# Two transformer blocks on one core: attention weights kept in plain float32 and applied to two heads side by side

## The chip, the cores and the metric

The kernel runs on one core of one Trainium2 chip. The metric is the device time of one execution in microseconds (us), as the median of three runs: 1866.72 us (1866.5 to 1867.96). Engines are named as in the profile: PE is TensorE's matmul stream and PEld its weight loads, DVE is VectorE, ACT is ScalarE, POOL is GpSimd, SP issues DMAs.

## The reference, cut to what matters

A sequence of 512 positions with 1024 features goes through two blocks. All inputs are float32. The change touches the places where attention weights meet values:

```python
# block 1, mixer: 8 "Fox" heads of 64, 4 "Diff" heads of 128
p = softmax(where(causal, q @ k.T * scale + F_q - F_k, -inf))      # Fox, per head
o = p @ v                                                          # 512 x 64
p1 = softmax(q1 @ k1.T * scale + bias); p2 = softmax(q2 @ k2.T * scale + bias)
o = rms_norm((p1 - lam * p2) @ v) * g                              # Diff, 512 x 128
# then gates, output projection, and a mixture of 32 experts (top 2 of 8 in one of 4 groups)

# block 2, mixer: 8 "NSA" heads of 64 (4 share one key/value head) and 4 mLSTM heads of 128
o = g0 * softmax(q @ k_cmp.T + b) @ v_cmp \
  + g1 * softmax(q @ k_slc.T + b) @ v_slc \
  + g2 * softmax(q @ k_win.T + b) @ v_win                          # 31 compressed keys, 512, 512
w = exp(D - m) * (q @ k.T);  h = (w @ v) / max(|sum w|, exp(-m))   # mLSTM, causal, 512 x 128
# then output projection, cross-attention to 256 memory tokens, and a gated feed-forward layer
```

## The kernel before

**Products.** Most matrix products run in the type float32r (`F32R`); such a product shows in the profile as one record. To come near float32, an operand is split in two: `hi` is the value rounded to float32r (an ACT instruction, L138), `lo` is the rest (a DVE subtraction, L145, which has to wait for `hi`). `mm3` (L152 to L154) then adds three products: hi·hi, hi·lo and lo·hi. A plain float32 operand needs no split; its product shows in the profile as two records for one instruction of the code. `hidden` (L804) issues 2 x 8 x 2 = 32 plain float32 products for each of 16 expert blocks, so 512, and its group on the page counts 1024.

**Attention.** A head works in four blocks of 128 queries; block `i` has keys 0 to 128(i+1). `softmax_rows` (L237, L239) leaves rows `sx` (queries on partitions). `transposer` (L254) turns them: for key block `j` it transposes the 4-j row blocks into one PSUM tile `tr` of 512, 384, 256 or 128 columns, and splits that into `pTh` and `pTl`. `finish` then applies them to the values. A Fox or NSA head (L441, L1489) puts the split values side by side (`v` hi in columns 0 to 63, lo in 64 to 127) as the stationary operand and streams `pTh` and `pTl` of each `j`: eight products of 512, 512, 384, 384, 256, 256, 128 and 128 columns. The result has the hi part on PSUM partitions 0 to 63 and the lo part on 64 to 127, so ACT copies one half out (`ou`), DVE adds the other, and the sum is split for the output projection (`oah`/`oal`, `yAh`/`yAl`). A Diff or mLSTM head (L475/L477, L1786/L1788) has 128-wide values; for each (i, j) one product streams 256 columns (hi and lo values) and a second 128, and ACT copies one half (`on`), DVE adds the other.

**Order.** Block 1's attention is a loop over head groups in which softmax blocks of one head, transposes of the head before and units of the next head's projection (`fill`) alternate. Block 2's is `run_tasks`: a task is one NSA head with one branch (`b` = 0 selected, 1 window), 16 in all, then four mLSTM cells. The NSA accumulator `o` is opened in `finish` of branch 0 (compressed branch first, L1483, then selected) and closed by branch 1. A scheduler in the framework then sets each engine's order; engines run theirs strictly in order. PSUM has four `mm` tiles, two `sc` (scores) and two `tr` (transposes). In block 2's attention stage the `lo` part of projection weights (`wl`, L219) and the mLSTM's convolution (`cy`, `mq`) run on POOL. mLSTM starts with `sel`, four small DVE copies (L1730) that a product (L1751) needs.

**Stages of the trace that the change touches** (us from the span's start): Fox 85 to 171, Diff 171 to 258, NSA 1090 to 1246, mLSTM 1246 to 1312.

Of the kernel before, what the change touches and what calls it, by code (L numbers as in the profile page):

```python
# [94 lines left out]
class Builder:  # L95
# [218 lines left out]
    def mixer1(self, x_dram, outer, before_gates, before_out):  # L314
        nc, tc, a = self.nc, self.tc, self.a
        w_in = a["w_in"][0]
        with ExitStack() as st:
# [10 lines left out]
            va = big.tile([P, NT, 8, 2, 64], F32R, tag="va_ob", name="va")  # L328
# [15 lines left out]
            with ExitStack() as sa:  # L344
# [75 lines left out]
                class Fox:  # L420
# [13 lines left out]
                    def finish(s, pT):  # L434
                        h, rr = s.h, slice(64 * s.r, 64 * s.r + 64)
                        o = ps.tile([P, S], F32, tag="mm", name="mm")
                        for j in range(NT):
                            sg = slice(self.SEG[j], self.SEG[j] + S - P * j)
                            v = va[:, j, h].rearrange("p a d -> p (a d)")
                            for m in range(2):  # L440
                                nc.tensor.matmul(o[:, P * j:], lhsT=v, rhs=pT[m][:, sg], start=j + m == 0,  # L441
                                                 stop=j == NT - 1 and m == 1)
# [1539 lines left out]
```

## Time and profile before

| | us |
|---|---|
| median of three runs | 1866.72 |
| the profiled execution's own time | 1868.54 |
| its span (first to last instruction) | 1866.7 |
| PE busy / PEld busy | 1768.0 / 1249.7 |
| DVE busy / ACT busy / POOL busy | 892.3 / 632.1 / 101.2 |
| mean granted TensorE clock | 0.976 of 2.4 GHz |

The span is 1.8 us shorter than the execution's own time; the profiled execution is 1.8 us longer than the median. "Busy" of an engine is the union of its records. A matmul record lasts longer than the engine needs for it: neighbours overlap, so rates are read from start to start, or from a group's union of busy time divided by its count. Over the whole span PE is busy 95% and DVE 48%; in the four stages above DVE is busy 64 to 90% of the time and ACT 47 to 81%.

### The profile page before, as it was taken

The numbers are of one execution on the slowest core, as the hardware profiler recorded it, in microseconds if no ns is written. First come the engines' busy times: TensorE is split into PE (matmuls) and PEld (weight loads), VectorE is DVE, ScalarE is ACT, GpSimd is POOL, SyncE is SP. The second block draws the span as 40 slices with busy tenths as digits, with TensorE's granted clock in tenths as the row PEclk, the third lists the DMA queues.
The fourth block names the chain that finished last, engine by engine and source line by source line (L and its number), as shares of the span: only waits on it lengthen the run. The fifth ranks groups of instructions, "written<-read, shape, count | busy, mean of one in ns | idle before, by whom it ended". The sixth has DMA issues, their size and how long they took to land. (4 is left out here: it accounts for less than half of the span.)

```text
span 1866.7 us, 22058 instructions
## 1 busy us (share of the span) xinstructions
PE 1768.0 (95%) x8295; PEld 1249.7 (67%) x8295; DVE 892.3 (48%) x2194; ACT 632.1 (34%) x1235; POOL 101.2 (5%) x100
## 2 busy tenths in 40 slices
PE   7999999999999999999998998889999999999998
PEld 5677777887655343333337876657787798888886
DVE  6499964335412221212107678866675553333224
ACT  4387742322100000000005568654354432323221
POOL 0000000011000000000001034200000000000000
PEclk9999999999999999999999999888999999999999
DMA  6322245346799999999977431101332233332321
GB/s 209 79 59 55 57 167 165 100 167 249 280 411 416 416 416 416 416 417 414 417 294 239 142 96 40 46 29 66 104 114 79 63 108 97 95 102 91 101 92 45
DMA packets 188987, 343.78 MB, mean 184 GB/s; under 512 B 14324, under 2 KB 136661, under 8 KB 172110
## 3 DMA queue, kind: packets, MB, share of 16 engines
q1 hardware_dynamic: 174768, 309.49, 45.9%
q0 software_dynamic: 8080, 25.07, 3.8%
q10 hardware_dynamic: 6030, 7.78, 1.2%
q8 instruction: 66, 1.08, 0.2%
q14 instruction: 43, 0.35, 0.1%
HBM read 330.74 MB, written 18.37 MB: 187 GB/s over the span
## 5 line engine op out<-in xcount | busy, mean ns | idle before, releaser
L219 DVE TENSOR_TENSOR wl<-wr,wh 128x1024 fp32r<-128x1024 f32 (+1 forms) x167 | 202.1, 1212 | 290.8 <-ACT wh L138 288.4
L138 ACT ACTIVATE wh<-wr 128x1024 fp32r<-128x1024 f32 (+1 forms) x178 | 185.9, 1050 | 434.0 <-PE mm L153 188.5
L152 PE MATMUL mm<-hTh,wh 128*128 128x512 f32 (+1 forms) x832 | 328.7, 395 | 0.0
L153 PE MATMUL mm<-hTl,wh 128*128 128x512 f32 (+1 forms) x832 | 322.8, 388 | 0.0
L154 PE MATMUL mm<-hTh,wl 128*128 128x512 f32 (+1 forms) x832 | 321.1, 386 | 0.4 <-DVE wl L219 0.4
L804 PE MATMUL mm<-we,xs 128*64 128x512 f32 x1024 | 241.4, 594 | 0.0
L154 PEld LDWEIGHTS mm<-hTh,wl 128*128 128x128 f32 x832 | 159.3, 191 | 29.9 <-DVE wl L219 0.8
L152 PEld LDWEIGHTS mm<-hTh,wh 128*128 128x128 f32 x832 | 159.1, 191 | 30.0 <-issue 3.8
L804 PEld LDWEIGHTS mm<-we,xs 128*64 128x64 f32 x1024 | 89.9, 137 | 129.3 <-issue 125.2
L153 PEld LDWEIGHTS mm<-hTl,wh 128*128 128x128 f32 x832 | 159.5, 192 | 24.4 <-issue 0.7
L856 PE MATMUL sc<-we,hT 128*64 128x512 f32 x512 | 142.3, 606 | 1.7 <-issue 1.7
L842 DVE SCALAR_TENSOR_TENSOR h<-mm,rsl,h 128x512 f32<-128x512 f32 x16 | 12.0, 750 | 178.8 <-PE mm L804 178.8
L856 PEld LDWEIGHTS sc<-we,hT 128*64 128x64 f32 x512 | 45.6, 138 | 76.8 <-issue 71.6
L239 ACT ACTIVATE sx<-sx,mn 128x384 f32<-128x384 f32 (+3 forms) x128 | 71.3, 557 | 23.9 <-DVE mn L237 23.5
L859 ACT COPY yt<-sc 128x512 f32<-128x512 f32 x16 | 9.4, 585 | 196.2 <-PE sc L856 196.2
L145 DVE TENSOR_TENSOR pTl<-tr,pTh 128x512 fp32r<-128x512 f32 (+3 forms) x136 | 66.3, 494 | 13.7 <-ACT pTh L138 13.3
L138 ACT ACTIVATE pTh<-tr 128x512 fp32r<-128x512 f32 (+3 forms) x136 | 59.0, 441 | 37.4 <-PE tr L254 31.6
L254 PE MATMUL tr<-ident,sx 128*128 128x128 f32 x320 | 62.3, 286 | 8.3 <-DVE pTl L145 4.9
L770 DVE TENSOR_TENSOR xg<-tr,gmoe 128x512 f32<-128x512 f32 x32 | 22.1, 690 | 97.8 <-PE tr L768 97.8
L254 PEld LDWEIGHTS tr<-ident,sx 128*128 128x128 f32 x320 | 40.4, 144 | 23.9 <-DVE pTl L145 8.9
L768 PE MATMUL tr<-x1h,oh 128*128 128x512 f32 x128 | 53.9, 421 | 0.3 <-DVE xs L792 0.3
L792 ACT COPY xs<-tr 128x512 f32<-128x512 f32 x16 | 9.4, 586 | 130.5 <-PE tr L780 130.4
(616 smaller groups left out, 3085.8 us busy)
## 6 DMA issues: line engine op xcount, KB each, us to landing
we<-in_w_dram SPq DMA_DIRECT2D x126, 1024.0 KB, 15.0
we<-in_w_dram SPq DMA_DIRECT2D x132, 512.0 KB, 14.3
wr<-in_w_in_dram SPq DMA_DIRECT2D x60, 512.0 KB, 3.9
wr<-in_w_gate_up_dram SPq DMA_DIRECT2D x44, 512.0 KB, 3.8
wr<-in_w_down_dram SPq DMA_DIRECT2D x22, 512.0 KB, 3.4
wr<-in_w_o_dram SPq DMA_DIRECT2D x8, 512.0 KB, 3.2
wr<-in_w_xkv_dram POOLq DMA_DIRECT2D x8, 512.0 KB, 7.7
yc<-ybuf SPq DMA_DIRECT2D x8, 512.0 KB, 8.4
```

The costliest lines, as they stand in the source:

```text
L138: self.nc.scalar.activation(out, src, AF.Copy if isinstance(scale, float) else AF.Identity, scale=scale)
L145: nc.vector.tensor_sub(lo, src, hi.bitcast(F32))
L152: mm(out, lhsT=lhs[0], rhs=rhs[0], start=start, stop=False)
L153: mm(out, lhsT=lhs[0], rhs=rhs[1], start=False, stop=False)
L154: mm(out, lhsT=lhs[1], rhs=rhs[0], start=False, stop=stop)
L219: next(self.lo_engines).tensor_sub(lo, raw, hi.bitcast(F32))
L239: nc.scalar.activation(s[:, :n], s[:, :n], AF.Exp, bias=mn, scale=-1.0, accum_out=rs)
L254: nc.tensor.transpose(pt[:, (i - j) * P:(i - j + 1) * P], rows[i][:, j * P:(j + 1) * P], self.ident)
L768: nc.tensor.matmul(pt, lhsT=oh[:, t], rhs=self.x1[m][:, t, c], start=t + m == 0, stop=t == NT - 1 and m == 1)
L770: nc.vector.tensor_mul(xg[:, c], pt, self.gmoe[:, c])
L804: self.nc.tensor.matmul(z[rr], lhsT=xs[:, k, rr], rhs=we[4 * m + 2 * (k // 4) + r][k % 4], start=k == 0, stop=k == KC - 1)
L856: nc.tensor.matmul(zs[hf][rr], lhsT=hT[:, k, rr], rhs=we[8 + 2 * (k // 2) + r][k % 2][:, hf * 512:hf * 512 + 512], start=k == 0, stop=k == 3)
```

## The change

The two mixers drop the split of the attention weights and of the values.

- `transposer32` copies each `tr` tile once, as float32, into `pT`: on ACT for j = 0 and 2, on DVE for j = 1 and 3. `pTh`, `pTl` and their eight split instructions a head go.
- The values `va`, `vb`, `vs`, `vc`, `mv` are copied once in float32.
- Fox and NSA: `finish` of an even head only keeps its `pT`. `finish` of the odd head calls `apply_pair`: for each `j` two plain float32 products with a stationary operand of 128 x 64, the even head's into PSUM partitions 0 to 63 and the odd head's into 64 to 127 of one tile. The tile is split for the output projection as it stands; `ou` and its addition go. The compressed branch does the same (`cp`, 31 x 64).
- Diff and mLSTM: one plain float32 product of 128 columns for each (i, j); the `on` copy and addition go (Diff scales from PSUM; mLSTM copies on DVE).
- `pT` has 3 buffers in block 1, 4 in NSA, 2 in mLSTM (before, `pTh` and `pTl` had 2 each).

```diff
+    def transposer32(self, rows, pool, ps, bufs):
+        nc = self.nc
+        out = pool.tile([P, 1280], F32, tag="pT", name="pT", bufs=bufs)
+        def step(j):
+            n = S - P * j
+            pt = ps.tile([P, S], F32, tag="tr", name="tr")
+            for i in range(j, NT):
+                nc.tensor.transpose(pt[:, (i - j) * P:(i - j + 1) * P], rows[i][:, j * P:(j + 1) * P], self.ident)
+            (nc.scalar.copy, nc.vector.tensor_copy)[j % 2](out[:, self.SEG[j]:self.SEG[j] + n], pt[:, :n])
+        step.out = out
+        return step
+
+    def apply_pair(self, o, vs, pTs, start=True, stop=True):
+        for j in range(NT):
+            for r in range(2):
+                self.nc.tensor.matmul(o[64 * r:64 * r + 64, P * j:], lhsT=vs[r](j),
+                                      rhs=pTs[r][:, self.SEG[j]:self.SEG[j] + S - P * j], start=start and j == 0,
+                                      stop=stop and j == NT - 1)
...
-            va = big.tile([P, NT, 8, 2, 64], F32R, tag="va_ob", name="va")
+            va = big.tile([P, NT, 8, 64], F32, tag="va_ob", name="va")
...
                     for t in range(NT):
-                        z = accs[t].rearrange("p (h d) -> p h d", d=wide)
-                        self.split(v[:, t, :, 0], v[:, t, :, 1], z)
+                        (nc.scalar.copy, nc.vector.tensor_copy)[t % 2](
+                            v[:, t], accs[t].rearrange("p (h d) -> p h d", d=wide))
...
                     def finish(s, pT):
-                        h, rr = s.h, slice(64 * s.r, 64 * s.r + 64)
+                        pTs = s.box.setdefault("pT", [])
+                        pTs.append(pT)
+                        if s.r == 0:
+                            return
                         o = ps.tile([P, S], F32, tag="mm", name="mm")
-                        for j in range(NT):
-                            sg = slice(self.SEG[j], self.SEG[j] + S - P * j)
-                            v = va[:, j, h].rearrange("p a d -> p (a d)")
-                            for m in range(2):
-                                nc.tensor.matmul(o[:, P * j:], lhsT=v, rhs=pT[m][:, sg], start=j + m == 0,
-                                                 stop=j == NT - 1 and m == 1)
-                        u = wk.tile([64, S], F32, tag="on", name="ou", bufs=1)
-                        nc.scalar.copy(u, o[64:])
-                        nc.vector.tensor_add(u, o[:64], u)
-                        self.split(oa[0][rr, h // 2], oa[1][rr, h // 2], u)
+                        self.apply_pair(o, [lambda j, h=s.h + r - 1: va[:, j, h] for r in range(2)], pTs)
+                        self.split(oa[0][:, s.h // 2], oa[1][:, s.h // 2], o)
...
                                 c0 = self.SEG[j] + P * (i - j)
-                                nc.tensor.matmul(o[:, :2 * P], lhsT=aT[0][:, c0:c0 + P],
-                                                 rhs=vb[:, j, h].rearrange("p a d -> p (a d)"), start=j == 0, stop=False)
-                                nc.tensor.matmul(o[:, :P], lhsT=aT[1][:, c0:c0 + P], rhs=vb[:, j, h, 0],
-                                                 start=False, stop=j == i)
-                            nc.scalar.copy(on[:, i], o[:, P:2 * P])
-                            nc.vector.tensor_add(on[:, i], o[:, :P], on[:, i])
-                            nc.vector.tensor_scalar_mul(on[:, i], on[:, i], s.inv1[:, i:i + 1])
+                                nc.tensor.matmul(o[:, :P], lhsT=aT[:, c0:c0 + P], rhs=vb[:, j, h], start=j == 0,
+                                                 stop=j == i)
+                            nc.vector.tensor_scalar_mul(on[:, i], o[:, :P], s.inv1[:, i:i + 1])
...
-                            trs = self.transposer(prev.rows, wk, pst)
+                            trs = self.transposer32(prev.rows, wk, pst, 3)
...
-                    hi = wk.tile([31, S], F32R, name="cph", bufs=1)
-                    lo = wk.tile([31, S], F32R, name="cpl", bufs=1)
-                    self.split(hi, lo, pt[:31])
-                    s.head["pc"] = (hi, lo)
+                    s.head["pc"] = wk.tile([31, S], F32, name="cp", bufs=3)
+                    nc.scalar.copy(s.head["pc"], pt[:31])
...
                 def finish(s, pT):
+                    s.pT = pT
+                    if s.h % 2 == 0:
+                        return
+                    heads = (tasks[2 * s.h - 2 + s.b], s)
                     if s.b == 0:
                         o = s.head["o"] = ps.tile([P, S], F32, tag="mm", name="mm")
-                        v = vc[:, s.g].rearrange("p a d -> p (a d)")
-                        for m in range(2):
-                            nc.tensor.matmul(o, lhsT=v, rhs=s.head["pc"][m], start=m == 0, stop=False)
+                        for r, t in enumerate(heads):
+                            nc.tensor.matmul(o[64 * r:64 * r + 64], lhsT=vc[:, s.g], rhs=t.head["pc"], start=True,
+                                             stop=False)
                     o = s.head["o"]
...
+                    self.apply_pair(o, [lambda j: vs[:, j, 2 * s.b + s.g]] * 2, [t.pT for t in heads], False, s.b == 1)
                     if s.b == 1:
-                        u = wk.tile([64, S], F32, tag="sx", name="ou", bufs=SN)
-                        nc.scalar.copy(u, o[64:128])
-                        nc.vector.tensor_add(u, o[0:64], u)
-                        rr = slice(64 * (s.h % 2), 64 * (s.h % 2) + 64)
-                        self.split(yA[0][rr, s.h // 2], yA[1][rr, s.h // 2], u)
+                        self.split(yA[0][:, s.h // 2], yA[1][:, s.h // 2], o)
...
-            self.run_tasks(tasks, 1.25, 0, wk, pst, before)
+            self.run_tasks(tasks, 1.25, 0, wk, pst, before, 4)
...
-                        nc.tensor.matmul(o[:, :2 * P], lhsT=aTr[0][:, c0:c0 + P],
-                                         rhs=mv[:, j, h].rearrange("p a d -> p (a d)"), start=j == 0, stop=False)
-                        nc.tensor.matmul(o[:, :P], lhsT=aTr[1][:, c0:c0 + P], rhs=mv[:, j, h, 0],
-                                         start=False, stop=j == i)
-                    nc.scalar.copy(on[:, i], o[:, P:2 * P])
-                    nc.vector.tensor_add(on[:, i], o[:, :P], on[:, i])
+                        nc.tensor.matmul(o[:, :P], lhsT=aTr[:, c0:c0 + P], rhs=mv[:, j, h], start=j == 0, stop=j == i)
+                    nc.vector.tensor_copy(on[:, i], o[:, :P])
```

Line numbers differ in the changed kernel; its transposes are L269, its copies L270, `apply_pair` L280, the compressed product L1500, its `sel` L1739 and the product that reads it L1760.

**Order, first place.** PE at the end of a Fox head, kernel before: the eight products of one head (`pTh`, `pTl` with `va`) stand together, behind a unit of projection and ahead of the next head's scores (`ka`, `kb`).

```order
L441 MATMUL mm<-pTh,va 128x512
L441 MATMUL mm<-pTl,va 128x512
L441 MATMUL mm<-pTh,va 128x384
L441 MATMUL mm<-pTl,va 128x384
L441 MATMUL mm<-pTh,va 128x256
L441 MATMUL mm<-pTl,va 128x256
L441 MATMUL mm<-pTh,va 128x128
L441 MATMUL mm<-pTl,va 128x128
L416 MATMUL sc<-ka,qa_243 128x128
```

The same place in the changed kernel, at the end of the first odd head ("x2" is the even head's product and then the odd head's):

```order
L154 MATMUL mm<-hTh,wl 128x512
L280 MATMUL mm<-pT,va 64x512 x2
L280 MATMUL mm<-pT,va 64x384 x2
L280 MATMUL mm<-pT,va 64x256 x2
L280 MATMUL mm<-pT,va 64x128 x2
L440 MATMUL sc<-ka,qa_243 128x128
L440 MATMUL sc<-kb,qb 128x128
```

All four Fox pairs stand together like this, and so do three of the four window pairs of NSA.

**Order, second place.** PE in NSA, the compressed and selected branch of one head, kernel before (`cph`/`cpl` with `vc`, then `pTh`/`pTl` with `vs`; `kk` are scores):

```order
L1483 MATMUL mm<-cph,vc 128x512
L1483 MATMUL mm<-cpl,vc 128x512
L1489 MATMUL mm<-pTh,vs 128x512
L1489 MATMUL mm<-pTl,vs 128x512
L1489 MATMUL mm<-pTh,vs 128x384
L1489 MATMUL mm<-pTl,vs 128x384
L1489 MATMUL mm<-pTh,vs 128x256
L1455 MATMUL sc<-kk_7065,qs 128x128
L1455 MATMUL sc<-kk_7066,qs 128x128
L152 MATMUL mm<-hTh,wh 128x512
L1489 MATMUL mm<-pTl,vs 128x256
```

The selected branch of the second pair in the changed kernel (`vt` and `ce` are transposes of other work):

```order
L1500 MATMUL mm<-cp,vc 64x512 x2
L280 MATMUL mm<-pT,vs 64x512
L1396 MATMUL tr<-ident,vt 128x128 x4
L269 MATMUL tr<-ident,sx 128x128 x2
L280 MATMUL mm<-pT,vs 64x512
L280 MATMUL mm<-pT,vs 64x384 x2
L280 MATMUL mm<-pT,vs 64x256
L1459 MATMUL tr<-ident,ce 31x128 x4
L269 MATMUL tr<-ident,sx 128x128
L280 MATMUL mm<-pT,vs 64x256
L280 MATMUL mm<-pT,vs 64x128
L1468 MATMUL sc<-kk_6859,qs 128x128
```

Other work stands between the even head's and the odd head's product of the same columns. Over all of NSA this happens twelve times: six times at 512 columns (two of them in L1500), once at 384, twice at 256, three times at 128.

**Order, third place.** DVE from the end of NSA into mLSTM, kernel before (`pTl` is the last split, `qkl` the split of queries and keys):

```order
L145 TENSOR_TENSOR pTl<-tr,pTh 128x128
L1494 TENSOR_TENSOR ou<-mm,ou 64x512
L145 TENSOR_TENSOR yAl<-ou,yAh 64x512
L1727 TENSOR_SCALAR gnorm<-vec 128x4
L1730 COPY sel<-ident 4x128 x4
L147 SCALAR_TENSOR_TENSOR qkl<-mq,qkh 128x512 x4
```

and the changed kernel:

```order
L270 COPY pT<-tr 128x384
L270 COPY pT<-tr 128x128
L1736 TENSOR_SCALAR gnorm<-vec 128x4
L1739 COPY sel<-ident 4x128 x4
L145 TENSOR_TENSOR yAl<-mm,yAh 128x512
L147 SCALAR_TENSOR_TENSOR qkl<-mq,qkh 128x512 x4
```

`sel` now stands ahead of the last head's output split. On PE, where L1751 followed the last NSA product at once, 18 projection products (six units of L152 to L154) now stand between that product and L1760. PE's, DVE's and ACT's order outside the two attention parts and the first few projection products stays as it was, as does SP's but for two weight loads that stand one place later; POOL's has one `wl` a few places earlier.

## Rows read from the trace of the kernel before

**Rows 1.** Windows: Fox, Diff, NSA, mLSTM; busy by engine, PEclk, DMA share, GB/s.
```profile
85.00:171.00 86.00, 81.99 (x419) 65.59 (x418) 77.06 (x207) 69.94 (x154) 0.00 (x0) 1.00 0.22 56
171.00:258.00 87.00, 80.87 (x401) 63.51 (x401) 74.93 (x277) 58.37 (x165) 0.00 (x0) 0.96 0.24 70
1090.00:1246.00 156.00, 136.65 (x741) 106.33 (x739) 134.13 (x397) 114.02 (x285) 46.94 (x29) 0.97 0.16 45
1246.00:1312.00 66.00, 64.72 (x265) 43.75 (x265) 42.03 (x151) 31.04 (x88) 3.33 (x7) 0.79 0.19 70
```

**Rows 2.** Waits of PE in NSA (us in total, times, longest).
```profile
PE mm L1489 <- DVE pTl L145: 7.1, 6, 2.2
PE tr L254 <- DVE pTl L145: 4.1, 4, 2.4
```

**Rows 3.** Groups by form, DVE: xcount | busy us, mean ns | idle before, releaser.
```profile
L145 DVE TENSOR_TENSOR pTl<-tr,pTh 128x512 fp32r<-128x512 f32 x40 | 27.2, 685 | 8.9 <-ACT pTh L138 8.6
...
L145 DVE TENSOR_TENSOR pTl<-tr,pTh 128x256 fp32r<-128x256 f32 x32 | 13.2, 414 | 1.0 <-ACT pTh L138 1.0
...
L849 DVE COPY hT<-tr 128x512 f32<-128x512 f32 x16 | 11.0, 688 | 10.1 <-PE tr L847 10.1
...
L145 DVE TENSOR_TENSOR yAl<-ou,yAh 64x512 fp32r<-64x512 f32 x8 | 7.6, 949 | 1.1 <-ACT yAh L138 1.0
...
L1494 DVE TENSOR_TENSOR ou<-mm,ou 64x512 f32<-64x512 f32 x8 | 5.5, 682 | 5.7 <-ACT ou L1493 5.7
...
L480 DVE TENSOR_TENSOR on<-mm,on 128x128 f32<-128x128 f32 x16 | 4.4, 282 | 1.4 <-ACT on L479 1.4
```

**Rows 4.** Groups by form, ACT.
```profile
L138 ACT ACTIVATE pTh<-tr 128x384 fp32r<-128x384 f32 x32 | 15.4, 482 | 4.9 <-PE tr L254 4.8
...
L138 ACT ACTIVATE pTh<-tr 128x128 fp32r<-128x128 f32 x32 | 8.7, 271 | 10.7 <-PE tr L254 10.1
...
L138 ACT ACTIVATE yAh<-ou 64x512 fp32r<-64x512 f32 x8 | 5.0, 626 | 0.9 <-DVE ou L1494 0.7
...
L1493 ACT COPY ou<-mm 64x512 f32<-64x512 f32 x8 | 4.7, 582 | 5.3 <-PE mm L1489 5.3
...
L479 ACT COPY on<-mm 128x128 f32<-128x128 f32 x16 | 3.8, 262 | 0.6 <-PE mm L477 0.6
```

**Rows 5.** Timeline of PE, end of a Fox head: start, us, instruction.
```profile
165.57 0.39 PE L441 MATMUL mm<-pTh,va 128*128 128x512 f32 x1
165.80 0.39 PE L441 MATMUL mm<-pTl,va 128*128 128x512 f32 x1
...
166.67 0.27 PE L441 MATMUL mm<-pTl,va 128*128 128x128 f32 x1
```

**Rows 6.** Groups by form, PE: plain float32 at 64 and at 128 columns.
```profile
L804 PE MATMUL mm<-we,xs 128*64 128x512 f32 x1024 | 241.4, 594 | 0.0
...
L1266 PE MATMUL mm<-wr,we 128*128 128x512 f32 x32 | 14.4, 592 | 0.0
```

**Rows 7.** Timeline of PE, experts: change between 128*64 and 128*128.
```profile
657.59 0.59 PE L856 MATMUL sc<-we,hT 128*64 128x512 f32 x1
658.11 0.50 PE L768 MATMUL tr<-x1h,oh 128*128 128x512 f32 x1
...
659.38 0.39 PE L768 MATMUL tr<-x1l,oh 128*128 128x512 f32 x1
659.70 1.07 PE L856 MATMUL sc<-we,hT 128*64 128x512 f32 x2
```

**Rows 8.** Tile view of sx, DVE at L1470: count, min/median/max ns, first and last start.
```profile
L1470 DVE TENSOR_SCALAR sx<-sx,nrs x48: 275/470/2535, 1096.8 to 1238.1; 128x128 f32<-128x128 f32 x16, 128x256 f32<-128x256 f32 x16, 128x512 f32<-128x512 f32 x16
```

**Rows 9.** Waits of PE in mLSTM.
```profile
PE mm L1751 <- DVE sel L1730: 3.1, 1, 3.1
```

**Rows 10.** Windows: first two parts of mLSTM.
```profile
1246.00:1270.00 24.00, 23.48 (x52) 13.64 (x53) 10.36 (x31) 6.64 (x14) 0.00 (x0) 0.50 0.04 11
1270.00:1294.00 24.00, 23.85 (x120) 16.78 (x119) 17.05 (x61) 13.33 (x41) 0.00 (x0) 1.00 0.13 45
```

More of the change, by code (lines that the diff above doesn't have):

```diff
@@ L352, in mixer1 @@
                 aug_k = cc.tile([P, S], F32, name="aug_k")
-                vb = cc.tile([P, NT, 4, 2, P], F32R, name="vb")
+                vb = cc.tile([P, NT, 4, P], F32, name="vb")
                 def values(c0, v, wide):
@@ L525, in mixer1 @@
                         self.drain()
-                trs = self.transposer(prev.rows, wk, pst)
+                trs = self.transposer32(prev.rows, wk, pst, 3)
                 for j in range(NT):
@@ L1201, in post_norm, with run_tasks @@
         return done
-    def run_tasks(self, tasks, slots, more, wk, pst, before):
+    def run_tasks(self, tasks, slots, more, wk, pst, before, bufs):
         prev, self.credit = None, 0
@@ L1209, in run_tasks @@
                 cur.start()
-            trs = self.transposer(prev.rows, wk, pst) if prev is not None else None
+            trs = self.transposer32(prev.rows, wk, pst, bufs) if prev is not None else None
             for i in range(NT):
@@ L1285, in mixer2 @@
         mq = rp.tile([P, 4, S], F32, name="mq")
-        mv = rp.tile([P, NT, 4, 2, P], F32R, name="mv")
+        mv = rp.tile([P, NT, 4, P], F32, name="mv")
         with ExitStack() as sa:
@@ L1289, in mixer2 @@
             gates = cc.tile([P, NT, 24], F32, name="gates")
-            vs = cc.tile([P, NT, 4, 2, 64], F32R, name="vs")
+            vs = cc.tile([P, NT, 4, 64], F32, name="vs")
             kk = [[cc.tile([P, S], F32R, name="kk%d%d" % (b, m)) for m in range(4)] for b in range(2)]
             kcp = [cc.tile([P, 64], F32R, name="kcp%d" % m) for m in range(2)]
-            vc = cc.tile([31, 2, 2, 64], F32R, name="vc")
+            vc = cc.tile([31, 2, 64], F32, name="vc")
             tabs = [cc.tile([P, 896], F32, name="tab%d" % i) for i in range(2)]
@@ L1336, in mixer2 @@
                 nc.vector.tensor_copy(gi[:, t], accs[t][:, 256:288])
-                z = accs[t][:, 0:256].rearrange("p (g d) -> p g d", d=64)
-                self.split(vs[:, t, :, 0], vs[:, t, :, 1], z)
+                nc.scalar.copy(vs[:, t], accs[t][:, 0:256].rearrange("p (g d) -> p g d", d=64))
             nc.scalar.activation(gates, gi[:, :, 0:24], AF.Exp, scale=-1.0)
@@ L1381, in done @@
                         nc.tensor.transpose(pt[:, t * P:(t + 1) * P], vt[:, t * P:(t + 1) * P], self.ident)
-                    self.split(mv[:, :, h, 0], mv[:, :, h, 1], pt.rearrange("p (t d) -> p t d", d=P))
+                    nc.scalar.copy(mv[:, :, h], pt.rearrange("p (t d) -> p t d", d=P))
                 self.queue_proj(lambda: w, hT, ps, done)
@@ L1665, in compress @@
             ov = o[:31, :P].rearrange("p (g d) -> p g d", d=64)
-            self.split(out[:, :, 0], out[:, :, 1], ov)
+            nc.vector.tensor_copy(out, ov)
     def mlstm_gates(self, pool, keep, gi, out):
@@ L1811, in mlstm @@
         cells = [Cell(h) for h in range(4)]
-        self.run_tasks(cells, 1, 1, wk, pst, before)
+        self.run_tasks(cells, 1, 1, wk, pst, before, 2)
         cells[3].after()
```

6 lines of the change are left out of this document (removed).

## Prediction

> **What bounds the kernel now.** I read the busy times of the four stages first [rows 1]. In none of them is PE without idle time: 4.0 us in Fox, 6.1 in Diff, 19.4 in NSA, 1.3 in mLSTM (86.00 - 81.99 and so on). The reader is to see that DVE is nearly as full as PE in the first three (77.1, 74.9 and 134.1 us) and that the granted clock is 0.79 in mLSTM, against 0.96 to 1.00 elsewhere. Then the waits of PE in NSA: 11.2 of the 19.4 us end on `pTl`, the second half of a split [rows 2]. Then mLSTM: PE waits 3.1 us for `sel` [rows 9], and the 24 us from there on run at 0.50, that is 1.2 GHz, with PE busy 23.5 of them; the 24 after that run at 1.00, 2.4 GHz [rows 10]. So NSA waits on a chain through ACT and DVE, and mLSTM's first part is PE at half clock.
>
> **What goes from DVE and ACT.** One task's split costs DVE four subtractions; two of them become copies at the same price (688 ns for a 512-column copy out of PSUM, 685 for the subtraction), two go, those of 512 and 256 columns: 0.685 + 0.414 = 1.10 us [rows 3]. ACT keeps the 512 and 256 and loses the 384 and 128: 0.482 + 0.271 = 0.75 us [rows 4]. The output of a pair took DVE 2 x (0.68 + 0.68) and ACT 2 x (0.58 + 0.63); one split of 0.68 and 0.63 stays, so 2.04 and 1.8 us go [rows 3, 4]. By stage, DVE and ACT:
> - Fox, 8 tasks, 4 pairs: 8.8 + 8.2 = 17.0 us, and 6.0 + 7.2 = 13.2.
> - Diff, 4 tasks and 16 `on` additions of 0.28 and copies of 0.26: 4.4 + 4.5 = 8.9, and 3.0 + 4.2 = 7.2.
> - NSA, 16 tasks, 4 pairs, and the second halves of 8 `cpl` and 4 `mv` at the 512-column price: 17.6 + 8.2 + 8.2 = 34.0, and 12.0 + 7.2 = 19.2.
> - mLSTM, 4 cells: DVE 4.4 (the additions become copies), ACT 3.0 + 4.2.
> DVE falls by a quarter in NSA. The value copies before the heads save about as much again as one task each; projection products run beside them, so they count as nothing.
>
> **What changes on PE.** A Fox head's eight products now take from 165.57 to 166.67 and one more short one, 1.16 us; one of 512 columns starts 0.23 after the last [rows 5]. So a pair costs 2.32. The new form stands in the experts: 512 products of 128 x 64 by 512 columns fill 1024 records in 241.4 us, 0.47 us a product, while one with 128 columns takes two records of 14.4/32 = 0.45, 0.90 us [rows 6]. Two neighbouring halves of the array thus run side by side. A pair of 512 columns costs 0.94, and the 1280 columns of a pair of heads 2.36 us. Each change of shape costs 0.32 against 0.23 on the way in and 0.52 against about 0.45 on the way out [rows 7], 0.09 and 0.07, so 2.52 with both: 0.2 more than before, 0.8 over four Fox pairs. From below, with free changes of shape and a pair at the 0.90 of one full-width product, it would be 2.25, 0.07 less than before; from above, halves that do not overlap cost 1280/512 x 2 x 0.90 = 4.5.
>
> In NSA the order breaks twelve of these pairs. A broken pair costs one product more than a whole one: 6 x 0.9 + 0.66 + 2 x 0.45 + 3 x 0.22 = 7.6 us, and 24 changes of shape x 0.08 = 1.9. The eight pairs cost 8 x 0.2 = 1.6 more; the compressed branch, 16 products of 0.23 and eight detours into the 31-row shape at 0.16, 5.0, becomes four pairs of 0.94 and about 0.3, 4.1. PE's work in NSA grows by 7.6 + 1.9 + 1.6 - 0.9 = 10 us.
>
> A Diff or mLSTM step (i, j) streams 256 + 128 columns at 0.23 for 512, so at least 0.17 us; the new product has two records of 128 columns, 0.90/4 = 0.225 [rows 5, 6]. That is up to 0.05 more, over 40 steps 2 us in either stage, or nothing if steps this short took 0.225 before as well; I take nothing, as both stages have that much idle time or more slack at half clock.
>
> **What of it lies on the path, stage by stage.**
> Fox: PE idles 4.0 us, and DVE had 9 us to spare; with 17 less it is late less often. Half of the idle time, less 0.8 of PE work: -1, bounds -4 and +2.
> Diff: 6.1 us idle, and the last head has no projection beside it, so there each of its four `on` copies and additions, 0.54 us, stands on the chain: -2.2, and a `pT` ready 0.4 to 0.7 us earlier. I take -3, bounds -6 and +2.
> NSA: of the 11.2 us that end on `pTl` one wait of 2.4 [rows 2] is DVE held up elsewhere (a 128- to 512-column scaling that takes 0.275 to 2.535 us [rows 8]); I keep it and let 8.8 go. Of the other 8.2 us of idle time half goes with a quarter less on DVE: -4. PE's 10 us come on top, but the breaks are where the order puts other work because the odd head's `pT` is not there yet, so PE would have stood still in part of them; I count 7. Sum -6, bounds -19 (all idle gone, breaks free) and +10 (nothing gone).
> mLSTM: `sel` now stands on DVE ahead of the output split, `ou` and its addition are gone from the chain, and 18 projection products, 18 x 0.23 = 4.2 us, cover it on PE: the 3.1 us go. Without that stop I expect the clock to stay at 2.4 GHz. The 23.5 us of PE work at 0.50 would need 11.7 at 1.00; DVE's 10.4 us in that stretch fit into 12 only if nothing waits, so I take -8 of the 11.7. Together -11, bounds -15 and -1 (the clock falls all the same).
> [...]
>
> Sum: -1 - 3 - 6 - 11 = -21. The profiled execution takes 1868.54 us, 1.8 over its span and 1.8 over the median; 1868.5 - 21 = 1847.5, and less 1.8 for the median 1845.7. I predict 1846.
>
> **The rivals.**
> 1. The clock falls in mLSTM anyway. For it: Diff and NSA have lowered stretches too (0.96 and 0.97 [rows 1]), and NSA's longest waits in these rows are 2.2 and 2.4 us [rows 2]. Against it: plain float32 products keep PE busy longer there than before. It takes back the 8 us: 1854.
> 2. NSA stays as long as it is, because DVE is held up by single slow instructions, not by its load. For it: 2.535 us where 0.275 is possible [rows 8]; POOL is busy 46.9 us in that stage [rows 1]. Against it: 11.2 us of PE's idle time end on an instruction that the change removes. NSA +4 instead of -6: 1856. [...]
> 3. Slower: the two halves of a pair do not run side by side here, since their stationary operands change with every product. Each pair of heads then costs 4.5 in place of 2.36. Fox: 4 x 2.2 more PE work on a PE whose idle 4 us end on other things, +8. NSA: the breaks cost nothing more, but eight pairs cost 2.2 more each and four compressed ones up to 0.9: 10 - 7.6 + 17 + 2 = 21, less the 8.8 of `pTl` waits, +12. With Diff's -3 and mLSTM's -11 the sum is +6: 1873. It decides once the odd half starts more than 0.4 us after the even one. Against it: the experts change both operands with every product too, and pay 0.47 [rows 6].
> 4. More: without the wait at each tile, PE runs NSA with little idle (-17) and Fox loses its 4 us: 1832.
>
> **How the numbers follow.** Forecast 0.45, its own range 1837 to 1853; the clock 0.2; NSA unchanged 0.13, and with the clock too 0.05 (1864); slower 0.1; more 0.07. Leaving out the slower case and the top of the double one, the range is 1830 to 1865. What this kernel's runs can tell from no change is 0.2%, 3.7 us. Faster by more has all cases that end below 1863: 0.83; within it, part of the double case and the edge of the slower one, 0.07; slower 0.10.
>
> **What the profile after would show.** The two halves of an `apply_pair` product start within some ns and the pair takes 0.9 us at 512 columns; in NSA the split ones 0.9 each. DVE in NSA near 100 us, ACT near 95, PE's need up by 10. No wait for `sel`, and PEclk near 1.00 in mLSTM, which ends within some 55 us. Stages outside the four keep their lengths. Wrong it is if PE idles as much in NSA as before, if the clock in mLSTM stands at 0.5, or if a pair takes 1.8.

## The result, and the profile after

The changed kernel takes 1840.27 us (four runs, 1837.61 to 1842.04) against 1866.7 us: a ratio of 0.9854, 95% interval [0.984, 0.9867], 26.4 us faster. The forecast was 1846, 20.7 us faster, with a range of 1830 to 1865. The profiled execution has a span of 1840.3 us against 1866.7.

The stages are cut here at the last product of Fox and of NSA, since the change also moves projection work from one stage to the next. First the kernel before, then the changed one; the columns are those of [rows 1]: Fox, Diff, NSA, mLSTM.

```profile
85.00:183.40 98.40, 94.04 (x479) 75.28 (x478) 88.79 (x252) 78.67 (x177) 0.00 (x0) 1.00 0.21 54
183.40:258.10 74.70, 68.92 (x343) 53.92 (x342) 63.20 (x233) 49.64 (x142) 0.00 (x0) 0.95 0.25 75
1090.00:1243.40 153.40, 136.62 (x741) 106.33 (x739) 132.90 (x395) 112.81 (x283) 46.94 (x29) 0.97 0.15 42
1243.40:1313.60 70.20, 65.69 (x272) 44.61 (x272) 44.52 (x159) 33.18 (x94) 3.81 (x7) 0.81 0.23 80
```

```profile
85.40:177.80 92.40, 91.72 (x473) 68.59 (x471) 76.17 (x223) 66.59 (x150) 0.00 (x0) 1.00 0.22 58
177.80:246.60 68.80, 65.54 (x349) 51.57 (x348) 56.97 (x210) 44.40 (x117) 0.00 (x0) 1.00 0.23 65
1082.00:1225.40 143.40, 132.54 (x727) 93.68 (x725) 100.78 (x344) 96.66 (x239) 47.17 (x29) 0.96 0.15 45
1225.40:1286.00 60.60, 60.60 (x282) 42.39 (x282) 39.89 (x136) 27.56 (x68) 2.75 (x5) 0.89 0.22 77
```

Fox and Diff together fall from 173.1 to 161.2 us, NSA from 153.4 to 143.4, mLSTM from 70.2 to 60.6. Some is given back: the gates behind Diff take 144.7 us instead of 142.0, the work behind mLSTM 1.2 more, and 1.2 in all is lost in block 1's start and ahead of NSA. -11.9 - 10.0 - 9.6 + 5.1 = -26.4. DVE in NSA stands at 100.8 us (132.9 before) and ACT at 96.7 (112.8); "near 100" and "near 95" were forecast. Over the four stages PE's idle time (the length less its busy time) falls from 31.4 to 14.8 us, by 16.6, and the time at a granted clock of 0.50 from 44.4 to 23.9 us, worth another 10 if half of it is counted as lost: 26.8 of the 31.5 us. That half is an estimate, here and below: products of 512 columns that follow one another start 0.43 us apart at 0.50 (before, from 1249.12) and 0.23 at 1.00 (after, from 1227.78), a little less than twice.

A pair of Fox heads on PE, timeline (start, duration, instruction), with the product ahead of it and the one behind it:

```profile
114.38 0.39 PE L154 MATMUL mm<-hTh,wl 128*128 128x512 f32 x1
114.70 2.37 PE L280 MATMUL mm<-pT,va 128*64 128x512 f32 x16
117.00 0.33 PE L440 MATMUL sc<-ka,qa 128*128 128x128 f32 x1
```

The 16 records of the pair take 2.30 us from start to start, and the way in 0.32 for 0.23. With both changes of shape that is 2.39, against 2.32 for two heads before [rows 5] and 2.52 in the forecast. So the two halves of a pair do run side by side, the second starting 6 ns behind the first (single records at 114.697 and 114.703), and the slower case is out.

One broken pair in NSA, same view:

```profile
1147.76 1.07 PE L1500 MATMUL mm<-cp,vc 31*64 31x512 f32 x4
1148.77 1.07 PE L280 MATMUL mm<-pT,vs 128*64 128x512 f32 x2
1149.77 0.66 PE L1396 MATMUL tr<-ident,vt 128*128 128x128 f32 x4
1150.27 0.38 PE L269 MATMUL tr<-ident,sx 128*128 128x128 f32 x2
1150.58 1.72 PE L280 MATMUL mm<-pT,vs 128*64 128x512 f32 x8
1152.22 0.62 PE L1459 MATMUL tr<-ident,ce 128*31 128x128 f32 x4
```

The even head's 512 columns run alone, 1.00 us with the change to the shape of the transposes. But from 1150.58 the odd head's 512, both 384 and the even head's 256 take 1.64 us together: 896 columns in the odd half beside 640 in the even one, where a whole pair takes 2.30 x 896/1280 = 1.61 for 896 in both. The late half runs its old product while the other has gone on to its next one: single records of the trace put the start of the odd head's 512 columns at 1150.577 and that of the even head's 384 at 1150.584. Here the break at 512 columns thus costs its 1.00 us once, and those behind it are partly caught up.

Waits of PE in NSA after (us in total, times, longest), against [rows 2]:

```profile
PE sc L1468 <- DVE mn L237: 3.6, 3, 2.5
PE tr L1459 <- DVE ce L1452: 2.9, 3, 1.6
PE tr L269 <- ACT sx L1481: 2.5, 2, 1.5
PE tr L269 <- DVE pT L270: 1.6, 1, 1.6
```

The 11.2 us on `pTl` are gone, and 10.6 us stand on other instructions: scores' minima `mn`, the compressed branch's `ce`, scalings `sx`, the copy `pT`. On `mn` PE had waited 2.3 us and on `ce` 1.2 before as well.

mLSTM after in three windows:

```profile
1225.40:1233.00 7.60, 7.60 (x31) 5.13 (x31) 5.40 (x11) 4.86 (x9) 0.00 (x0) 1.00 0.14 38
1233.00:1246.70 13.70, 13.70 (x31) 7.56 (x30) 5.39 (x17) 3.61 (x8) 0.00 (x0) 0.50 0.10 38
1246.70:1286.00 39.30, 39.30 (x222) 29.70 (x223) 29.10 (x109) 19.09 (x52) 2.75 (x5) 1.00 0.28 97
```

No wait for `sel` is left; PE is busy for all of the 60.6 us. Yet the granted clock stands at 0.50 for 13.7 of them, where [rows 10] had 24. What PE did before it fell, from NSA's last transposes on:

```profile
1222.57 0.55 PE L269 MATMUL tr<-ident,sx 128*128 128x128 f32 x3
1223.05 2.37 PE L280 MATMUL mm<-pT,vs 128*64 128x512 f32 x14
1225.34 0.49 PE L152 MATMUL mm<-hTh,wh 128*128 128x512 f32 x1
...
1229.41 0.40 PE L154 MATMUL mm<-hTh,wl 128*128 128x512 f32 x1
1229.74 1.12 PE L1760 MATMUL mm<-aT,sel 4*128 4x512 f32 x2
...
1232.70 0.54 PE L152 MATMUL mm<-hTh,wh 128*128 128x512 f32 x1
1233.04 0.62 PE L153 MATMUL mm<-hTl,wh 128*128 128x512 f32 x1
```

The product at 1233.04 lasts 0.62 us, where one like it took 0.40 at 1229.41. No transpose stands between NSA's last ones, at 1222.57, and the fall.

### The profile page after: what moved, and what is told of

Read it like the earlier page. It is cut to its first block, busy times and chain, and to the rows that moved or that the text cites. A ratio compares the mean times of both kernels' runs of the same rounds, so it can differ in the third digit from the quotient of the medians.

```text
span 1840.3 us, 21813 instructions
## 1 busy us (share of the span) xinstructions
PE 1754.1 (95%) x8295; PEld 1226.6 (67%) x8295; DVE 834.3 (45%) x2070; ACT 590.9 (32%) x1110; POOL 101.5 (6%) x100
## 5 line engine op out<-in xcount | busy, mean ns | idle before, releaser
L152 PE MATMUL mm<-hTh,wh 128*128 128x512 f32 (+1 forms) x832 | 327.9, 395 | 0.7 <-ACT wh L138 0.7
L154 PE MATMUL mm<-hTh,wl 128*128 128x512 f32 (+1 forms) x832 | 318.7, 383 | 0.6 <-DVE wl L219 0.6
L154 PEld LDWEIGHTS mm<-hTh,wl 128*128 128x128 f32 x832 | 158.1, 190 | 31.0 <-DVE wl L219 1.1
L152 PEld LDWEIGHTS mm<-hTh,wh 128*128 128x128 f32 x832 | 158.2, 190 | 30.2 <-issue 3.3
L269 PE MATMUL tr<-ident,sx 128*128 128x128 f32 x320 | 60.5, 282 | 5.0 <-ACT sx L1481 2.5
L269 PEld LDWEIGHTS tr<-ident,sx 128*128 128x128 f32 x320 | 41.7, 144 | 23.2 <-ACT sx L1481 3.2
L784 PE MATMUL tr<-x1l,oh 128*128 128x512 f32 x128 | 51.7, 404 | 0.0
L876 DVE COPY yt<-sc 128x512 f32<-128x512 f32 x16 | 11.1, 691 | 76.8 <-PE sc L872 76.8
```

The lines of the kernel that those rows point to most:

```text
L152: mm(out, lhsT=lhs[0], rhs=rhs[0], start=start, stop=False)
L154: mm(out, lhsT=lhs[1], rhs=rhs[0], start=False, stop=stop)
L269: nc.tensor.transpose(pt[:, (i - j) * P:(i - j + 1) * P], rows[i][:, j * P:(j + 1) * P], self.ident)
L784: nc.tensor.matmul(pt, lhsT=oh[:, t], rhs=self.x1[m][:, t, c], start=t + m == 0, stop=t == NT - 1 and m == 1)
```

## The experiments

**Which stage gives what.** Three kernels carry one part of the change each: block 1's attention, block 2's mixer, and NSA alone.

```diff
+            va = big.tile([P, NT, 8, 64], F32, tag="va_ob", name="va")        # va, vb, Fox and Diff
+            self.run_tasks(tasks, 1.25, 0, wk, pst, before, 4)                # NSA and
+        self.run_tasks(cells, 1, 1, wk, pst, before, 2)                       # mLSTM
+            self.run_tasks(tasks, 1.25, 0, wk, pst, before, 4)                # NSA alone
```

Each comes with the lines of the change that belong to it.

> Only block 1's attention (Fox, Diff) is changed; block 2 stays as it was. Theory: the gain of each block stands for itself. In the traces the changed block 1 ends 11.9 us earlier, of which the gates give 2.8 back: 1866.7 - 9 = 1858. Rival: the 2.8 us lost in the gates belong to a clock that falls once in any case, so the gain of block 1 alone is 6 or less, or 12: 1861 or 1855.

Measured 1860.95, ratio 0.9965 [0.9952, 0.9977]: 6.5 us, 4.3 to 9.0. Its profile ends the gates 8.4 us early, mLSTM 9.6 and the program 8.5. The rival's gain of 6 fits as well as the theory's 9; its 12 is out.

> Only block 2's mixer (NSA, mLSTM) is changed. Theory: NSA and mLSTM together end 19.6 us earlier than before in the traces, of which 1.2 are given back by 1320: 1866.7 - 18 = 1849. Rival: block 2 gains only because it starts under another clock history: under 14 us, 1853 or more.

Measured 1848.6, ratio 0.9904 [0.987, 0.9938]: 17.9 us, 12 to 24. The four executions lie at 1841.59, 1843.95 (mean granted clock 0.985) and 1853.25, 1853.68 (0.978): how long the clock is down differs between executions of one kernel, and that goes with some 10 us. The theory's 18 us is met by the median, but the interval does not shut out the rival's 14. The two parts add up to 24.4, which agrees with the whole's 26.4 within their intervals.

> Only NSA is changed (weights once, pairs); Fox, Diff and the mLSTM cells stay as they were. Theory: NSA's own part is about 13 us (its stretch 158.5 to 141.0 us with 18 products moved out of it, 4.2), and the stop before mLSTM goes with it, since the output split is what sel stood behind: with the fall in mLSTM 1852, without it 1843. Rival, of the prediction: NSA's own part is 6: 1849 to 1860.

Measured 1849.93, ratio 0.9905 [0.9889, 0.992], 17.7 us: as much as all of block 2, and within the rival's range. In its profile NSA alone takes 143.8 us from its first scores to its last product on the values, against 152.6 before; 12 projection products moved out (2.8 us) are part of that, so NSA's own part is 6, as the rival has it, 3.4 of them the clock (3.4 us at 0.50 in place of 10.2). The larger rest lies behind NSA, where PE no longer waits for `sel`. What the mLSTM cells themselves save cannot be read from the medians, since the kernel with all of block 2 spreads over 12 us. In the two profiles, each with 6.8 us at 0.50 in NSA and mLSTM, these stages take 203.8 us without the changed cells and 197.1 with them, so it is some 6 us.

**The stop ahead of mLSTM.** The kernel before, with nothing changed but:

```diff
-        sel = cc.tile([4, 4, P], F32, name="sel")
-        for h in range(4):
-            nc.vector.tensor_copy(sel[:, h], self.ident[:4, h:h + 1].to_broadcast([4, P]))
...
-                nc.tensor.matmul(s.ab, lhsT=sel[:, s.h], rhs=aT, start=True, stop=True)
+                nc.tensor.matmul(s.ab, lhsT=self.ident[:4, s.h:s.h + 1].to_broadcast([4, P]), rhs=aT,
+                                 start=True, stop=True)
```

> The kernel before, with mLSTM's row product reading the identity's column by a broadcast, so that PE no longer waits 3.1 us for sel. Theory of the prediction: the stop also brought the clock down; without it 3.1 + 8 us go: 1856. Rival: the clock falls in mLSTM all the same, as it does for 13.7 us in the changed kernel without any wait: only the 3.1 us and the shorter fall go, at most (24 - 14)/2 = 5 more, 1858 to 1864; if nothing of the fall goes, 1863.5.

Measured 1851.74, ratio 0.9917 [0.99, 0.9933]: 15.5 us, 12 to 19, so the rival is out. The windows of NSA and mLSTM:

```profile
1085.00:1240.50 155.50, 139.81 (x738) 108.76 (x737) 132.10 (x393) 112.70 (x281) 47.25 (x29) 0.95 0.14 41
1240.50:1294.20 53.70, 52.10 (x273) 38.13 (x272) 44.18 (x155) 32.96 (x95) 3.81 (x7) 1.00 0.26 90
```

mLSTM runs at 1.00, but the clock stands at 0.50 for 10.2 us late in NSA (1218.9 to 1229.1), where the kernel before has no fall. Over both stages, 209.2 us for 223.6, the time at 0.50 goes from 37.5 to 17.1 us: the 3.1 us of the stop and half of these 20.4 are 13.3 of the 14.4. One wait of 3.1 us was thus worth more than half of what the whole change brings; its share and the clock's cannot be told apart by the medians.

> The changed kernel, with mLSTM's row product over 128 rows (124 of them zero) in place of 4, in the same time. Theory: the clock falls 3.3 us after the first such product because PE has little to do in those 1.1 us; with all rows it stays at 2.4 GHz in mLSTM, -5 to -7: 1834. Rival: it is the short products with 64 rows, or NSA's end before it; the clock falls all the same, 1840.

```diff
+        aT = keep.tile([P, S], F32, name="aT")        # was [4, S]; rows 4 to 127 zero
+        nc.vector.memset(aT, 0.0)
...
+            nc.vector.tensor_copy(sel[:, h], self.ident[:, h:h + 1].to_broadcast([P, P]))
```

Measured 1834.67, ratio 0.9824 [0.9807, 0.9841]. Its mLSTM has no fall:

```profile
1227.70:1281.50 53.80, 53.80 (x282) 39.12 (x282) 39.62 (x135) 27.38 (x68) 2.74 (x5) 1.00 0.23 84
```

That is what was expected, but the row product stayed as it was in two kernels below, those with the odd head first and with `wl` on DVE, and their mLSTM windows stand at 0.97 and 1.00. So it is not shown that the four rows bring the fall.

**Load or chain.** After each copy out of `tr`, the other engine reads the tile once more, for nobody:

```diff
+            if j % 2 == 0:
+                nc.vector.tensor_sub(dead[:, :n], pt[:, :n], out[:, self.SEG[j]:self.SEG[j] + n])
+            else:
+                nc.scalar.copy(dead[:, :n], pt[:, :n])
```

> The changed kernel, with the split's second half put back as work that nobody reads: DVE subtractions of 512 and 256 columns and ACT copies of 384 and 128, per transposed head. It loads DVE with 1.10 us a head again (17.6 in NSA, half of what it saves there) and holds the PSUM tile as long as before; PE waits for none of it. Theory, load: half of the gain outside mLSTM's start goes, +8 to +12, 1850. Rival, chain: what counted was that a product waited for ACT and then DVE; 0 to +3, 1841 to 1843.

Measured 1849.17, ratio 0.9892 [0.9874, 0.991]: 7 to 9 us of the gain are given back, by the ratios and by the medians. Its NSA:

```profile
1087.70:1242.00 154.30, 142.03 (x739) 98.46 (x737) 116.25 (x376) 105.63 (x271) 46.82 (x29) 0.94 0.14 42
```

DVE has 15.5 us more than in the changed kernel, and the stage is 10.9 us longer. The loss is near what the load theory gave and well over the chain theory's 0 to 3. How it comes about is not shown: of the 10.9 us, 3.0 are 13 projection products that stand in NSA and not behind it, 3.4 are the clock (17.1 us at 0.50 for 10.2), and PE idles only 1.4 us more (12.3 for 10.9). Nor does the run separate DVE's time from the longer hold of the two `tr` tiles.

**Pairs.** All four products of the even head first, then the odd head's:

```diff
-        for j in range(NT):
-            for r in range(2):
+        for r in range(2):
+            for j in range(NT):
```

> The changed kernel, with all four products of the even head ahead of the four of the odd head, so that the halves of the array do not run side by side. In the trace after, a product of 512 columns takes 1.0 us alone and a pair of them 0.94, so a pair of heads costs 1280/512 x 1.0 x 2 = 5.0 against 2.3. Theory, PE is the bound in Fox and NSA: 12 pairs x 2.6 less what breaks already cost, +22 to +30, 1862 to 1870. Rival, PE has idle time to put it in (5 us in block 1, 11 in NSA): +10 or less, 1850.

Measured 1852.02, ratio 0.9911 [0.9895, 0.9928], 11 us slower than with pairs. One pair of heads:

```profile
115.85 3.93 PE L280 MATMUL mm<-pT,va 128*64 128x512 f32 x16
119.70 0.33 PE L440 MATMUL sc<-ka,qa 128*128 128x128 f32 x1
```

3.85 us for 2.30; 5.0 was too high, since the edit does not part the heads altogether: in the trace the odd head's first product starts at 117.41, beside the even head's last 256 and 128 columns. A product of 512 columns with nothing beside it takes 0.91 us here (115.85 to 116.76), and a pair of them in the changed kernel takes 0.91 too (114.70 to 115.61). Summed from each record's start to the next one's, these products (the compressed ones with them) take 55.8 us in both stages against 39.8. The stages, Fox with Diff, NSA and mLSTM:

```profile
86.60:253.80 167.20, 163.27 (x819) 123.29 (x818) 133.69 (x432) 110.60 (x267) 0.00 (x0) 1.00 0.21 59
1087.00:1239.70 152.70, 142.52 (x723) 96.58 (x721) 100.53 (x344) 96.61 (x239) 47.06 (x29) 0.97 0.14 42
1239.70:1295.00 55.30, 55.30 (x285) 39.82 (x285) 39.91 (x136) 27.45 (x68) 2.74 (x5) 1.00 0.24 82
```

Fox and Diff are 6.0 us longer than in the changed kernel and NSA 9.3, so nearly all of the 16 us stand in these stages: PE's idle time, 10.2 us in NSA for 10.9, hides next to none of them, and the rival is wrong. The whole is 11 us slower and not 16, since mLSTM gives 5.3 back (55.3 us for 60.6): the clock does not fall there in this profile, and the mean granted clock of the four executions is 0.983 to 0.987, of the changed kernel's 0.980 to 0.983. So the theory's price was twice too high, but the loss does lie in PE's time on these products, 16.0 us more by their starts.

```diff
-            for r in range(2):
+            for r in (1, 0):
```

> The changed kernel, with the odd head's product ahead of the even head's in each pair: the one that waits comes first, and the pairs of NSA stand together but for one. Theory, the breaks cost what they take: each broken 512-column pair 1.0 us, the shorter ones 0.4 to 0.7, about -4: 1836. Rival: the odd head's weights are late and PE stands still, or the other half catches up by running its next product beside it: 0, 1840.

Measured 1835.41, ratio 0.9822 [0.9807, 0.9838], the 4 us expected, but not from the step named. The pair products in NSA take 27.0 us from start to start instead of 30.6. The stage:

```profile
1082.50:1225.20 142.70, 129.51 (x731) 91.91 (x729) 103.00 (x344) 96.28 (x239) 46.81 (x29) 0.96 0.15 45
```

142.7 us for 143.4, with six projection products (1.4 us) more in it: most of what PE saves it now waits (13.2 us idle for 10.9). The gain in this profile lies in mLSTM, where the clock fell for 3.4 us in place of 13.7. So the rival is nearly right on NSA, and that the forecast came true is luck.

**POOL beside DVE.** One line of both kernels:

```diff
-            self.share(0, 1)
+            self.share(1, 0)
             self.run_tasks(tasks, 1.25, 0, wk, pst, before, 4)
```

> The changed kernel, with the low part of NSA's projection weights on DVE in place of POOL. Theory: POOL's long instructions hold up DVE's scalings (2.5 us where 0.28 is possible), and DVE now has 42 of 143 us free, so the waits of PE in NSA shrink: -3 to -5, 1836. Rival: DVE gets 1.2 us more per weight, some 25 us, and is late with scores and weights again: +3 or more, 1843.

Measured 1824.17, ratio 0.9769 [0.9754, 0.9785]: 16 us faster than the changed kernel, four times what was expected. NSA, to be compared with 143.40 us of the changed kernel:

```profile
1079.50:1213.60 134.10, 128.92 (x729) 92.17 (x728) 99.52 (x353) 96.65 (x239) 26.21 (x20) 0.99 0.16 48
```

DVE in NSA by groups, first of the changed kernel, then with `wl` on DVE:

```profile
L1483 DVE TENSOR_SCALAR sx<-sx,nrs 128x128 f32<-128x128 f32 (+2 forms) x48 | 23.9, 525 | 0.7
L270 DVE COPY pT<-tr 128x384 f32<-128x384 f32 (+1 forms) x32 | 13.4, 420 | 13.3 <-PE tr L269 13.2
L1477 DVE TENSOR_TENSOR nrs<-nrs,gates 128x2 f32<-128x2 f32 x32 | 10.8, 337 | 0.6
...
L1452 DVE TENSOR_TENSOR ce<-ce,csm 128x124 f32<-128x124 f32 x8 | 4.1, 516 | 0.2
```

```profile
L1483 DVE TENSOR_SCALAR sx<-sx,nrs 128x128 f32<-128x128 f32 (+2 forms) x48 | 18.7, 415 | 0.6
L270 DVE COPY pT<-tr 128x384 f32<-128x384 f32 (+1 forms) x32 | 13.4, 419 | 9.8 <-PE tr L269 9.5
L219 DVE TENSOR_TENSOR wl<-wr,wh 128x1024 fp32r<-128x1024 f32 x9 | 12.0, 1337 | 7.3 <-ACT wh L138 7.2
L1477 DVE TENSOR_TENSOR nrs<-nrs,gates 128x2 f32<-128x2 f32 x32 | 8.1, 254 | 0.5
...
L1452 DVE TENSOR_TENSOR ce<-ce,csm 128x124 f32<-128x124 f32 x8 | 2.7, 336 | 0.1
```

and POOL's group of `wl` in the changed kernel:

```profile
L219 POOL TENSOR_TENSOR wl<-wr,wh 128x1024 fp32r<-128x1024 f32 x9 | 21.5, 2392 | 48.1 <-ACT wh L138 48.0
```

DVE takes on 12.0 us and its total goes from 100.8 to 99.5. The scalings, the products with the gates and one of `ce` get shorter (525 to 415, 337 to 254, 516 to 336 ns; the longest scaling 2456 to 1067); the copy out of PSUM does not (420, 419), and neither does the reciprocal of `nrs` (159, 161). On POOL a weight took 2392 ns, on DVE 1337. In the changed kernel's trace the six scalings of NSA that take more than 0.5 us, 0.83 to 2.46, all run while POOL works, and the 41 with nothing on POOL beside them take 487 ns at most; in the kernel before it is nine of 0.77 to 2.54, and 489 ns at most for 36.

Of the 17.5 us by which NSA and mLSTM together are shorter in this profile (186.5 for 204.0), 5.7 are idle time of PE (5.2 for 10.9) and 10.2 the clock, which is down for 3.4 us in place of 23.9. The mean granted clock of the five executions is 0.983 to 0.988, of the changed kernel's four 0.980 to 0.983. Why the clock is down for less is not shown.

> The kernel before, with the low part of NSA's projection weights on DVE in place of POOL, and nothing else. Theory, POOL holds up DVE: 9 weights cost DVE 9 x 1.34 = 12.0 us and free about as much (scalings, small products), so NSA gets 5 to 10 us shorter here too; the stop before mLSTM stays: 1858 to 1863. Rival: DVE is busy 134 of 156 us here, and only the changed kernel has the room: no gain or a loss, 1867 to 1872.

Measured 1851.49, ratio 0.9919 [0.9904, 0.9934]: 15.1 us, 12 to 18, more than expected; the rival is out. Its waits:

```profile
PE mm L1489 <- DVE pTl L145: 3.3, 5, 1.3
PE mm L1751 <- DVE sel L1730: 3.1, 1, 3.1
...
PE tr L254 <- DVE pTl L145: 1.1, 3, 0.5
```

The waits on `pTl` fall from 11.2 to 4.4 us with the split still there, so most of that wait was not the split's. The longest scaling falls from 2535 [rows 8] to 1541 ns. The mean of the scalings falls from 560 to 480, so they are shorter with `wl` off POOL; but the order of NSA moves with this edit on every engine, and the 15 us are not all shown to be that. In the profiles NSA and mLSTM lose 8.1 us of PE's idle time, and the time at 0.50 falls from 37.5 to 13.7 us, worth 11.9, so more than half is the clock. The stop of 3.1 us is still there, but the clock behind it fell for 6.8 us in place of 24:

```profile
1235.00:1241.80 6.80, 5.73 (x11) 2.96 (x11) 4.53 (x12) 3.40 (x7) 0.00 (x0) 0.50 0.15 45
1241.80:1294.30 52.50, 51.08 (x255) 36.08 (x256) 38.60 (x143) 28.46 (x84) 3.80 (x7) 0.97 0.25 86
```

**Together.**

> The changed kernel with the odd head's product first, mLSTM's row product over 128 rows and the low weight parts of NSA on DVE. Theory: the three act in different places (PE's breaks, the clock in mLSTM, POOL beside DVE) and add up to what is left of them: lo on DVE gave 16, whose run had no fall in mLSTM any more, so the row product adds 0 and the order about 3: 1821. Rival: with POOL out of the way the pairs were whole in time anyway: 1824.

Measured 1821.47, ratio 0.9747 [0.9734, 0.9761]. The theory's 1821 and the rival's 1824 lie too near each other to be told apart by it.

The last kernel takes the convolution off POOL as well:

```diff
-                    nc.gpsimd.tensor_add(y[:, d:], y[:, d:], ct[:, d:])
+                    nc.vector.tensor_add(y[:, d:], y[:, d:], ct[:, d:])
-                nc.gpsimd.tensor_mul(u, u, y)
-                nc.gpsimd.tensor_add(u, u, y)
+                nc.vector.tensor_mul(u, u, y)
+                nc.vector.tensor_add(u, u, y)
```

> As the three together, with the 20 instructions of mLSTM's convolution on DVE as well, so that POOL does nothing in NSA. Theory, POOL holds up DVE: 26 us of POOL go, DVE gets some 20 x 0.7 = 14 us more and frees as much or half of it; 0 to -3 against the three together, 1819. Rival: DVE becomes late with scores: +3, 1825.

Measured 1818.16, ratio 0.9733 [0.9717, 0.9749]; the last two cannot be told apart, both beat the changed kernel by some 20 us, and the rival's 1825 is out. NSA with nothing on POOL, and two of DVE's groups in it:

```profile
1083.80:1211.50 127.70, 127.33 (x728) 87.97 (x726) 102.74 (x373) 95.94 (x238) 0.00 (x0) 1.00 0.17 50
```

```profile
L1483 DVE TENSOR_SCALAR sx<-sx,nrs 128x128 f32<-128x128 f32 (+2 forms) x48 | 16.6, 371 | 0.4
L1477 DVE TENSOR_TENSOR nrs<-nrs,gates 128x2 f32<-128x2 f32 x32 | 5.0, 156 | 0.4
```

The scaling and the product with the gates, 525 and 337 ns in the changed kernel and 415 and 254 with `wl` on DVE, are now down to 371 and 156, so in these three kernels their time falls with each piece of work that leaves POOL. PE idles 0.4 us of 127.7. Here PE is the bound, and by that idle time less load on DVE would bring next to nothing more.

## Why the prediction was right, step by step

The total came out within 6 us of the forecast, and in part by luck: against -1 - 3 - 6 - 11 the profiles show -11.9 for Fox and Diff, -10.0, -9.6, and 5.1 us given back in stages that were to keep their lengths.

- **What goes from DVE and ACT**: right; both totals in NSA came within 2 us. The split of `yA` stands in the sum with 0.68 us where its row says 949 ns [rows 3]; reading PSUM now, it took 691 ns.
- **A pair on PE**: right, 2.39 us for 2.52. The bound of 4.5 belongs to halves that do not overlap; heads apart, which still overlap at one end, measured 3.85.
- **NSA, -6**: right by two errors that cancel. The stage fell by 10.0 us, of which 3.5 are 15 products (195 to 180 counted) that now run in mLSTM: -6.5. The idle time fell from 16.8 to 10.9 us, by 5.9 and not the 12.8 that I took: the waits on `pTl` went, and those on `mn`, `ce`, `sx` and `pT` grew. I had kept only one wait of 2.4 us as DVE held up elsewhere; in the kernel before with `wl` on DVE 6.8 of the 11.2 us went with POOL's weights alone. And PE's busy time fell by 4.1, 0.6 beyond the moved products, where I counted +7: breaks cost PE 3.6 us by the kernel with the odd head first, not 9.5, since a late half catches up beside the next product (896 and 640 columns in 1.64 us). Rival 2's single slow instructions fit what is left (scalings of up to 2456 ns, and 5.7 us of PE's idle time gone with `wl` on DVE), though they did not keep NSA from getting shorter.
- **mLSTM, -11**: right in size, half right in cause. With the moved products its stretch shrank by 9.6 + 3.5 = 13.1. The stop went, as its order had shown. That the clock then stays up failed in the profiled run: 13.7 us at 0.50, with PE busy throughout, which is one of the prediction's own signs of being wrong, and rival 1 in part. PE's idle time fell from 4.5 us (3.1 of them the stop) to nothing and the time at 0.50 from 27.3 us to 13.7: 4.5 + 6.8 = 11.3; the rest is about what is given back right behind mLSTM. In the kernel before without the wait for `sel` the clock held in mLSTM, but fell ahead of it.
- **Rival 1, the clock falls anyway**: in the profiled run it did, at 1233.0, with no wait of PE in mLSTM ahead of it. Of what PE ran before, transposes take 2.8 of NSA's last 10 us; the fall comes 10 us after the last of them, and 18 projection products, 4.2 us, stand between. No run here tells whether any of these matters.
- **Fox -1 and Diff -3**: too small, -11.9 in the profile. PE's idle time went from 10.1 to 3.9 us; I had let half of Fox's 4.0 and 3 of Diff's 6.1 go. 3.4 more are two falls of the clock in Diff (0.95 in its window) that did not occur, and the gates, with a longer fall than before (0.96 in place of 0.98) and 3.3 us more idle time, gave 2.7 back. By medians of the kernel with block 1 alone the part is worth 6.5, so the forecast of 4 was low by about as much as can be measured.

What stays open: why a stop of 3.1 us is followed by 24 us at 0.50 in the kernel before and by 6.8 in the same kernel with `wl` on DVE, and why the clock falls in mLSTM without any stop in some executions (13.7 us in the profile of the changed kernel, none in that of the heads apart). Behind the stop both kernels issue the same products for 5.6 us (the row product, six projection products, two products of scores); in the one the clock rises right after them, in the other it stays down for another 18 us. So what PE ran behind the stop does not settle it. That transposes or short products cause it was not tried apart.

## What to carry to other kernels

Look first for the one wait of some us ahead of a stretch of dense products: here it cost 15 us with the clock that fell behind it, and reading the operand by a broadcast removed it. Before an operation is taken off a loaded DVE, look at what POOL runs beside it: nine weight subtractions moved to DVE made DVE's total in NSA smaller in the changed kernel (100.8 to 99.5 us) and both kernels 15 us faster, more than half of it through the clock. Two 64-column plain float32 products, one into PSUM partitions 0 to 63 and one into 64 to 127, cost here what one of them does, 0.91 us at 512 columns, when they are issued together (a whole pair of heads takes 2.30 us, with the heads apart 3.85), and in the broken pair above the half that was late caught up beside the next product (1.64 us for 896 and 640 columns).

## What the runs showed of the hardware

- Two plain float32 products of 128 x 64 by 512 columns, one into PSUM partitions 0 to 63 and one into 64 to 127, take 0.91 us together (a pair of Fox heads in the changed kernel), one with nothing beside it 0.91 too (the heads apart).
- In a broken pair of NSA the odd head's 512 columns (start at 1150.577) ran beside the even head's 384 (1150.584); 896 columns in the one half and 640 in the other took 1.64 us.
- The granted clock stood at 0.50 for 13.7 us with PE busy for every one of them (changed kernel, 1233.0 to 1246.7), and executions of one kernel differ in it (block 2 alone: mean clock 0.985 at 1841.59 us, 0.978 at 1853.68).
- A subtraction of 1024 columns took 2392 ns on POOL and 1337 on DVE; DVE's scalings beside it took up to 2456 ns in the changed kernel (2535 in the kernel before), those with nothing on POOL beside them 487 at most (489).
